# RWKV dumps and chunk loads moved from ScalarE's queue to SyncE's in a hybrid transformer block

## The chip, the cores and the metric

The kernel runs on one core of one Trainium2 chip. The metric is the device time of one execution in microseconds (us). TensorE multiplies matrices, VectorE and ScalarE do elementwise work, GpSimd a little of it, and SyncE only starts transfers. ScalarE can start transfers too: such an instruction stands in its one stream of work, between its copies and activations. Each engine takes its instructions strictly in order.

## The reference

One transformer block over 512 tokens of width 1024, in float32. A normalised input is projected by `w_in` to the inputs of three mixers and their gates; the mixers' outputs are gated, merged and projected; a gated feed-forward follows. What matters here is the projection, which is most of the matmul work, and the second mixer, RWKV-7, with 16 heads of size 64:

```python
z = h @ w_cols
zq, zf, zi, zog, zrw, zcq, zckv, zkr, zgate, zvres = jnp.split(z, IN_SPLITS, axis=-1)
o_hg = hgrn2_mixer(zq, zf, zi, zog, ...)
o_rw, v_first = rwkv7_mixer(zrw, ...)
o_mla = mla_mixer(zcq, zckv, zkr, ...)

def step(state, inp):                     # inside rwkv7_mixer, scanned over the 512 tokens
    r_t, w_t, k_t, v_t, kk_t, a_t = inp
    sa = jnp.einsum('bhvk,bhk->bhv', state, -kk_t)
    state = (state * w_t[:, :, None, :] + sa[..., None] * (kk_t * a_t)[:, :, None, :]
             + v_t[..., None] * k_t[:, :, None, :])
    return state, jnp.einsum('bhvk,bhk->bhv', state, r_t)
```

## The kernel before

**The dense stream.** Every large product goes through `stream`. Weights come in slabs of two k-tiles by 256 columns (256 KB). `slab` loads one into `wsD` on SyncE's queue, ScalarE rounds it into `whD` (L207), and VectorE takes the rest into `wlD` (`split_low`, L134). TensorE then does twelve matmuls of 128x512 on it, three for each k-tile and column block (L139 to L141), into two PSUM tiles `mmD`. Four slabs make a group; after it ScalarE copies both tiles to `zst` (L239, or L253 for the gates), and SyncE stores them (`z` or `gth`). `wsD`, `whD` and `wlD` have three buffers each, `mmD` and `zst` two. GpSimd writes a tiny `token` after every three matmuls (L151), and TensorE may not run more than five tokens ahead.

**RWKV** fills the gaps of that stream. The sequence is cut into eight chunks of 64 tokens, the heads into eight pairs, and a group is two pairs. `rwkv_group` prepares one group in a tile `G` (two buffers): `rwkv_prep` for each pair (decay scan, normalised keys, chunk-wise products, masks, transposes), `rwkv_inverse` (a recursion on VectorE), and `rwkv_merge`, whose last copies are on ScalarE (L668). Then `G` is dumped to DRAM, into `rwd`, by four transfers on ScalarE's queue (L461 and L462): 2 x (2240 + 256) KB. The next user of that buffer of `G` begins with two memsets on GpSimd (L449), which wait until the dump has landed. `rwkv_chain` comes after the fourth group and goes through the chunks in order. Chunk `c` of all groups is loaded into a tile `CH` (three buffers) by four transfers of 640 KB on ScalarE's queue (L683), one for each group. In a chunk TensorE does the products `zus` (L701, L711, L717) and `yb` (L196, L725), with copies between them on VectorE and ScalarE.

**What sets the order.** The program is written in lanes, which are priorities: the dense stream's casts and evictions are in lane 0, the chain in lane 1, the other linear mixer (HGRN, tiles `ph`, `hq`, `hk`, `hz`) in lane 2 for its products, inverse, merge and dump in lane 3, and `rwkv_prep` in lane 5. A scheduler takes, for each engine, the ready instruction of the best lane by its own estimate of times, and so writes one fixed order for each engine. `issue_after` and `add_manual_dep` add edges that it has to keep.

Of the kernel before, what the change touches and what calls it, by code (L numbers as in the profile page):

```python
# [17 lines left out]
ALU = mybir.AluOpType  # L18
# [4 lines left out]
P = 128  # L23
# [13 lines left out]
NC = S // C  # L37
# [5 lines left out]
RWC = 5 * P  # L43
# [61 lines left out]
class Kern:  # L105
# [336 lines left out]
    def rwkv_group(self, g):  # L442

        all_ = self.t(self.gp, [P, 2, NC, RWC], "G", bufs=2)
        G = self.fields(all_)
        G["all"] = all_
        for e in range(2):

            self.nc.gpsimd.memset(G["PV"][e][e * 64:e * 64 + 64], 0.0)  # L449
        G["Ld"] = self.t(self.dpool, [64, 32, 32], "Ld", bufs=2)  # L450
        G["Td"] = self.t(self.dpool, [64, 32, 32], "Td", bufs=2)
        for q in range(2):
            self.lane(5)
            self.rwkv_prep(G, 2 * g + q, q)
        self.lane(3)
        self.rwkv_inverse(G, g)
        self.rwkv_merge(G, g)
        for q in range(2):
            to = self.rwd[g][:, :, q].rearrange("c p n -> p c n")

            self.nc.scalar.dma_start(to[:, :NC - 1], all_[:, q, :NC - 1])  # L461
            self.nc.scalar.dma_start(to[:, NC - 1, :RWC - P], all_[:, q, NC - 1, :RWC - P])  # L462

    def fields(self, t):

# [3 lines left out]
    def rwkv(self, e1, e2, e3):  # L469
        self.lane(5)  # L470
        self.rwkv_lora()
        for g in range(4):
            self.rwkv_group(g)
        e2.close()
        self.rw = e1.enter_context(self.tc.tile_pool(name="rwC", bufs=1, side="right"))
        self.lane(1)
        self.rwkv_chain()
# [11 lines left out]
    def rwkv_prep(self, G, p, q):  # L489
        nc, rt = self.nc, self.rt  # L490
        V, A, Pl = nc.vector, nc.scalar, nc.gpsimd
# [15 lines left out]
        def rate(ps, tag, b):  # L507
            x = self.t(rt, [P, S], tag)
            A.activation(x, ps, AF.Tanh, bias=b[:, p:p + 1], scale=0.5)
            return x  # L510

        t1 = rate(pl[0], "t1", self.hw0)
        a = rate(pl[1], "a", self.ha0)
        lw = self.t(rt, [P, NC, C + 1], "lw")
        Pl.memset(lw[:, :, 0:1], 0.0)
        A.activation(lw[:, :, 1:], c3(t1), AF.Copy, bias=-0.5 * DECAY, scale=-0.5 * DECAY)
        cs = self.t(rt, [P, NC, C + 1], "cs")
        V.tensor_tensor_scan(cs.rearrange("p c j -> p (c j)"), self.keep, lw.rearrange("p c j -> p (c j)"),
                             0.0, op0=ALU.mult, op1=ALU.add)
        V.tensor_tensor(lw, cs, cs[:, :, C:].to_broadcast([P, NC, C + 1]), op=ALU.subtract)  # L520
        ep = self.t(rt, [P, NC, C + 1], "cs")
        em = self.t(rt, [P, NC, C + 1], "em")
# [6 lines left out]
        def proj(n, tag):  # L529
            dst = self.t(rt, [P, S], tag)  # L530
            self.shifted(dst, 8 * n + p)
            return dst

        k = proj(1, "k")
        kk, sq = self.t(rt, [P, S], "lw"), self.t(rt, [P, S], "t1")
# [10 lines left out]
        pb = self.t(self.pR, [P, NT, P], "pr")  # L546
# [2 lines left out]
        for i in range(NT):  # L549
            nc.tensor.transpose(pb[:, i, :], rb[:, 2 * i:2 * i + 2].rearrange("t h d -> t (h d)"), self.ident)  # L550
        pb = pb.rearrange("p i t -> p (i t)")
        V.tensor_tensor(kk, kk, pb, op=ALU.mult)

        BK = self.t(rt, [P, NC, P], "BK")
        X = G["X"]
# [1 line left out]
            V.scalar_tensor_tensor(X[e][H[e], q, :, 0:C], c3(kk)[H[e]], -1.0, ep[H[e], :, 0:C], op0=ALU.mult, op1=ALU.mult)  # L557
        V.scalar_tensor_tensor(kk, a, 1.0, kk, op0=ALU.add, op1=ALU.mult)
        A.activation(a, a, AF.Identity, bias=self.omka[:, p:p + 1], scale=self.hka[:, p:p + 1])
        V.tensor_tensor(k, k, a, op=ALU.mult)  # L560
        for e in range(2):
            V.scalar_tensor_tensor(BK[H[e], :, e * C:(e + 1) * C], c3(kk)[H[e]], 0.5, em[H[e], :, 1:], op0=ALU.mult, op1=ALU.mult)
            V.tensor_tensor(BK[H[e], :, (1 - e) * C:(2 - e) * C], c3(k)[H[e]], em[H[e], :, 1:], op=ALU.mult)
# [21 lines left out]
        n = NC - 1  # L585
# [7 lines left out]
        v = proj(2, "v")  # L593
        rkk = self.t(rt, [P, S], "t1")
        V.scalar_tensor_tensor(rkk, r, self.vec("rwkv_r_k", p), k, op0=ALU.mult, op1=ALU.mult)
        ps = self.t(self.pR, [P, S], "pr")
# [2 lines left out]
        self.split_low(rl, rkk, rh)  # L599
        nc.tensor.matmul(ps, lhsT=self.bdR, rhs=rh, start=True, stop=False)  # L600
        nc.tensor.matmul(ps, lhsT=self.bdR, rhs=rl, start=False, stop=True)
        V.tensor_tensor(rkk, ps, v, op=ALU.mult)
        nc.sync.dma_start(self.bv[p], rkk)

        lh, ll = self.lora_w(((slice(0, P), ins["rwkv_g_up"][0, :, f]),))
        ps = self.t(self.pR, [P, S], "pr")
        self.mm3(ps, lh, ll, self.zg[:, 0], self.zg[:, 1], True, True)
        g = self.t(rt, [P, S], "v")
# [61 lines left out]
    def rwkv_chain(self):  # L670

        nc, rw = self.nc, self.rw
        V, A, Pl = nc.vector, nc.scalar, nc.gpsimd
        mm = nc.tensor.matmul
        H = [slice(0, 64), slice(64, 128)]
        heads = [(p, e) for p in range(8) for e in range(2)]
        chunks = []

        def load(c):
            t = self.t(rw, [P, 8, RWC], "CH", bufs=3)  # L680
            n = RWC if c < NC - 1 else RWC - P
            for g in range(4):
                nc.scalar.dma_start(t[:, 2 * g:2 * g + 2, :n], self.rwd[g][c][:, :, :n])  # L683
            chunks.append(self.fields(t))

        load(0)
        St = self.t(rw, [P, 8, C], "St")
        y = self.t(rw, [P, NT, 8, 2, C], "y")
        for c in range(NC):
            if c < NC - 1:  # L690
                load(c + 1)
            G = chunks[c]
            X, PV, LM, BKT = (G[n] for n in ("X", "PV", "LM", "BKT"))
            if 0 < c < NC - 1:

                for e in range(2):
                    Pl.tensor_tensor(St[H[e]], PV[e][H[e]], self.gC[H[e], :, c + 1:c + 2].to_broadcast([64, 8, C]), op=ALU.mult)
            yo = (H[c % 2], H[1 - c % 2])
            z = self.t(self.pC, [P, 8, C], "zus")
            for p, e in heads:  # L700
                mm(z[H[e], p, :], lhsT=X[e][:, p, 0:C], rhs=PV[e][:, p, :], start=True, stop=True)  # L701
            zsb = self.t(rw, [P, 8, C], "zsb")
            V.tensor_copy(zsb, z)
            yb = self.t(self.pY, [P, 8, C], "yb")

            self.side_by_side(
                partial(mm, yb[yo[e], p, :], lhsT=X[e][:, p, C:], rhs=PV[e][:, p, :], start=p == 0, stop=False)
                for p, e in heads)
            z = self.t(self.pC, [P, 8, C], "zus")
            for p, e in heads:  # L710
                mm(z[H[e], p, :], lhsT=LM[H[e], p, 0:C], rhs=zsb[H[e], p, :], start=True, stop=True)  # L711
            V.tensor_copy(PV[0][H[0]], z[H[0]])
            A.copy(PV[1][H[1]], z[H[1]])
            if c < NC - 1:
                z = self.t(self.pC, [P, 8, C], "zus")
                for p, e in heads:
                    mm(z[H[e], p, :], lhsT=BKT[:, p, H[e]], rhs=PV[e][:, p, :], start=True, stop=True)  # L717
                for e in range(2):
                    nxt = chunks[c + 1]["PV"][e][H[e]]
                    if c == 0:  # L720
                        V.tensor_copy(nxt, z[H[e]])
                    else:
                        V.tensor_tensor(nxt, z[H[e]], St[H[e]], op=ALU.add)
            for p, e in heads:
                mm(yb[yo[e], p, :], lhsT=LM[H[e], p, C:], rhs=PV[e][H[e], p, :], start=False, stop=p == 7)  # L725
            for e in range(2):
                A.copy(y[yo[e], c // 2, :, e, :], yb[yo[e]])
            if c % 2:
                self.lane(3)
                self.rwkv_norm(y[:, c // 2].rearrange("t p e d -> t (p e) d"))  # L730
                self.lane(1)
        self.lane(3)

        bv, gr, out = (self.t(rw, [P, 8, RWC], "CH", bufs=3) for _ in range(3))
        for p in range(8):
            nc.sync.dma_start(bv[:, p, :S], self.bv[p])
            nc.sync.dma_start(gr[:, p, :S], self.grw[p])
        for p in range(8):
            pt = self.t(self.pC if p % 2 else self.pY, [P, S], "zus" if p % 2 else "yb")
            for i in range(NT):  # L740
                nc.tensor.transpose(pt[:, i * P:(i + 1) * P], y[:, i, p].rearrange("t e d -> t (e d)"), self.ident)
            o = out[:, p, :S]
            o4 = o.rearrange("f (i j t) -> f i j t", j=2, t=C)
            pt4 = pt.rearrange("f (i j t) -> f i j t", j=2, t=C)
            lb, lg = self.vec("rwkv_lnx_b", p), self.vec("rwkv_lnx_g", p)
            A.activation(o[H[0]], pt[H[0]], AF.Identity, bias=lb[H[0]], scale=lg[H[0]])
            for j in range(2):

                A.activation(o4[H[1], :, j, :], pt4[H[1], :, 1 - j, :], AF.Identity, bias=lb[H[1]], scale=lg[H[1]])
            V.tensor_tensor(o, o, bv[:, p, :S], op=ALU.add)  # L750
            V.tensor_tensor(o, o, gr[:, p, :S], op=ALU.mult)
            nc.sync.dma_start(self.orw[p], o)
            self.dump(f"orw{p}", o)
# [591 lines left out]
```

## Time and profile before

| | us |
|---|---|
| median of 3 runs | 1435.62 (1430.45 to 1436.62) |
| the profiled execution | 1436.18 |
| its span | 1434.4 |
| TensorE busy | 1364.7 (95%) |
| VectorE, ScalarE, GpSimd busy | 853.0, 637.4, 166.4 |
| data moved | 235.80 MB, mean 164 GB/s |

The profiled execution lies 0.6 us above the median and takes 1.8 us more than its span. An engine that starts a transfer is not counted as busy: such a row bears the engine's name with a q (ACTq, SPq), and its duration is the time for which the instruction held the engine. The time to landing, from the issue until the data has arrived, is another number. In rows of waits there follow the total, the count and the longest. In rows of windows there follow each engine's busy time with its count of instructions, then the clock granted to TensorE (1.00 is full), the busy share of the 16 DMA engines and GB/s. Rows of a timeline or of the chain begin with the start and the duration; brackets give the engine's idle time before the instruction and what ended it.

### The profile page before, as it was taken

What the parts mean: (1) busy time and instruction counts of PE and PEld (TensorE: products, weight loads), DVE (VectorE), ACT (ScalarE), POOL (GpSimd) and SP (SyncE); (2) the same over time, 40 slices, a digit from 0 to 9 for tenths busy, and PEclk for the clock granted to TensorE, in tenths of its full rate; (3) what the DMA queues carried; (4) which work ended last, traced back from release to release, by engine and by line L of the source; (5) the groups of instructions that cost most, each with busy time, mean ns of one, the idle gap of its engine ahead of it and who ended that gap; (6) DMA issues with size and microseconds to landing.
All of it is one profiled execution on the core that took longest, in us unless ns stands there. A gap on an engine that the chain in (4) does not pass through costs nothing.

```text
span 1434.4 us, 27281 instructions
## 1 busy us (share of the span) xinstructions
PE 1364.7 (95%) x9664; PEld 1106.5 (77%) x9664; DVE 853.0 (59%) x1756; ACT 637.4 (44%) x1259; POOL 166.4 (12%) x1000
## 2 busy tenths in 40 slices
PE   7999998998999899799999999999999999999998
PEld 6777767676776677688787878887878888888886
DVE  5566887795887784365667366665465444443234
ACT  5563555555455443234565444453344333332222
POOL 3112112111111111132210000000010000000000
PEclk9999999999999999899999999999999999999999
DMA  6564466546654748887647465403645333335333
GB/s 191 145 183 130 136 175 234 169 149 207 212 167 136 250 142 272 329 275 257 224 143 234 133 191 158 156 25 126 205 134 149 99 96 96 96 97 158 97 96 103
DMA packets 186168, 235.80 MB, mean 164 GB/s; under 512 B 33840, under 2 KB 126512, under 8 KB 186032
## 3 DMA queue, kind: packets, MB, share of 16 engines
q1 hardware_dynamic: 171072, 190.02, 43.9%
q10 hardware_dynamic: 14960, 44.05, 8.3%
q8 instruction: 76, 1.25, 0.4%
q14 instruction: 60, 0.49, 0.1%
HBM read 171.75 MB, written 62.26 MB: 163 GB/s over the span
## 4 chain that ended last, share of the span: by engine, by line
PE 75%; DMA 9%; DVE 6%; ACT 4%; issue 3%; ACTq 1%; SPq 1%; POOL 0%; DVEq 0%; POOLq 0%
PE mmD L139 17%; PE mmD L140 16%; PE mmD L141 16%; PE po L140 4%; PE po L141 4%; PE po L139 4%; DMA z<-zst 1%; DMA hz<-z 1%; DMA rwd<-G 1%; DMA zr<-z 1%; PE pm L139 1%; PE pm L140 1%; PE pm L141 1%; PE pr L196 1%; PE pmo L1117 1%
## 5 line engine op out<-in xcount | busy, mean ns | idle before, releaser
L139 PE MATMUL mmD<-xH,whD 128*128 128x512 f32 (+1 forms) x1232 | 489.6, 400 | 20.7 <-ACT zst L239 6.3
L140 PE MATMUL mmD<-xL,whD 128*128 128x512 f32 (+1 forms) x1232 | 476.6, 388 | 0.0
L141 PE MATMUL mmD<-xH,wlD 128*128 128x512 f32 (+1 forms) x1232 | 471.7, 387 | 1.5 <-DVE wlD L134 1.4
L134 DVE TENSOR_TENSOR wlD<-wsD,whD 128x512 fp32r<-128x512 f32 x384 | 264.0, 690 | 303.9 <-ACT whD L207 285.5
L207 ACT CAST whD<-wsD 128x512 fp32r<-128x512 f32 x384 | 236.4, 618 | 352.7 <-PE mmD L140 206.5
L139 PEld LDWEIGHTS mmD<-xH,whD 128*128 128x128 f32 x1232 | 233.1, 190 | 74.7 <-issue 15.6
L141 PEld LDWEIGHTS mmD<-xH,wlD 128*128 128x128 f32 x1232 | 233.7, 190 | 50.3 <-DVE wlD L134 3.0
L140 PEld LDWEIGHTS mmD<-xL,whD 128*128 128x128 f32 x1232 | 235.1, 191 | 40.4
L151 POOL MEMSET token<- 1x1 f32 x912 | 82.1, 90 | 754.3 <-PE mmD L141 739.2
L141 PE MATMUL po<-whD,fL 128*128 128x512 f32 x176 | 68.6, 390 | 0.0
L140 PE MATMUL po<-wlD,fH 128*128 128x512 f32 x176 | 68.6, 390 | 0.0
L139 PE MATMUL po<-whD,fH 128*128 128x512 f32 x176 | 62.0, 390 | 0.0
L281 POOL TENSOR_TENSOR rrs<-rtm,mhalf 128x1 f32<-128x1 f32 x8 | 4.4, 550 | 402.3 <-DVE rtm L276 368.7
L636 DVE TENSOR_TENSOR invtmp<-inv 64x30 f32<-64x30 f32 (+14 forms) x120 | 39.7, 331 | 16.2 <-DMA inv<-Ld 14.3
L239 ACT COPY zst<-mmD 128x512 f32<-128x512 f32 x64 | 37.4, 584 | 15.8 <-PE mmD L141 15.5
L637 DVE TENSOR_TENSOR inv<-inv,invtmp 64x30 f32<-64x30 f32 (+14 forms) x120 | 38.4, 320 | 2.0
L139 PEld LDWEIGHTS po<-whD,fH 128*128 128x128 f32 x176 | 33.0, 188 | 7.1
L141 PEld LDWEIGHTS po<-whD,fL 128*128 128x128 f32 x176 | 33.0, 188 | 7.0
L140 PEld LDWEIGHTS po<-wlD,fH 128*128 128x128 f32 x176 | 33.0, 188 | 7.0
L822 PEld LDWEIGHTS ph<-hq,hk 128*32 128x32 f32 x1536 | 16.8, 112 | 18.3 <-issue 8.9
L1115 ACT COPY mpT<-pmt 128x128 f32<-128x128 f32 (+3 forms) x32 | 13.6, 425 | 29.2 <-PE pmt L1113 28.9
L1117 PEld LDWEIGHTS pmo<-mpT,mv 128*128 128x128 f32 x160 | 22.3, 191 | 4.7 <-ACT mpT L1115 2.6
(349 smaller groups left out, 1964.4 us busy)
## 6 DMA issues: line engine op xcount, KB each, us to landing
wsD<-in_w_in_dram SPq DMA_DIRECT2D x176, 256.0 KB, 3.1
wsD<-in_w_ffn_in_dram SPq DMA_DIRECT2D x96, 256.0 KB, 2.8
rwd<-G ACTq DMA_DIRECT2D x8, 2240.0 KB, 11.6
CH<-rwd ACTq DMA_DIRECT2D x28, 640.0 KB, 8.4
z<-zst SPq DMA_DIRECT2D x63, 256.0 KB, 3.2
wsD<-in_w_branch_dram SPq DMA_DIRECT2D x48, 256.0 KB, 3.0
wsD<-in_w_ffn_out_dram SPq DMA_DIRECT2D x44, 256.0 KB, 2.6
zr<-z SPq DMA_DIRECT2D x26, 256.0 KB, 3.5
```

Source lines behind the costliest of these rows:

```text
L134: (eng or self.nc.vector).tensor_tensor(dst, src, high.bitcast(F32), op=ALU.subtract)
L139: first = mm(ps, lhsT=lh, rhs=rh, start=start, stop=False)
L140: mm(ps, lhsT=lh, rhs=rl, start=False, stop=False)
L141: return first, mm(ps, lhsT=ll, rhs=rh, start=False, stop=stop)
L151: token = self.nc.gpsimd.memset(self.token, 0.0).ins
L196: last = c()
L207: nc.scalar.copy(h, st)
L239: self.nc.scalar.copy(st[:m], ps)
L636: V.tensor_tensor(tv, cv, rv, op=ALU.mult)
L637: V.tensor_tensor(U[:, :j, j + 1:], U[:, :j, j + 1:], tv, op=ALU.add)
L822: mm(g[b:b + HB, o // P, :], lhsT=k[:, t], rhs=q[:, t], start=True, stop=True)
L1117: mm(pq[:, t], lhsT=self.v[:, j, h, :], rhs=pT[:, j * P:(j + 1) * P], start=j == 0, stop=j == i)
```

## The change

The dump of a group is cut into its eight chunks, of 640 KB each (512 KB for the last), and goes to SyncE's queue. The chunks are put into a list. Four places of `rwkv_prep` (the decay scan, two products on the way to the keys, and the bonus product) take one chunk from the list and issue its transfer behind an edge from that VectorE instruction; two pairs make eight such places for each group. The fourth group has no successor, so its chunks are issued at once. The loads of the chain go to SyncE's queue as well. The bytes are the same.

```diff
         self.rwkv_merge(G, g)
-        for q in range(2):
-            to = self.rwd[g][:, :, q].rearrange("c p n -> p c n")
-
-            self.nc.scalar.dma_start(to[:, :NC - 1], all_[:, q, :NC - 1])
-            self.nc.scalar.dma_start(to[:, NC - 1, :RWC - P], all_[:, q, NC - 1, :RWC - P])
+        for c in range(NC):
+            n = RWC if c < NC - 1 else RWC - P
+            self.dumps.append((self.rwd[g][c][:, :, :n], all_[:, :, c, :n]))
+        if g == 3:
+            while self.dumps:
+                self.nc.sync.dma_start(*self.dumps.pop(0))
+
+    def dump_step(self, by):
+
+        if self.dumps:
+            cur = self.cur_lane
+            self.lane(3)
+            d = self.nc.sync.dma_start(*self.dumps.pop(0))
+            self.lane(cur)
+            self.tc.add_manual_dep(d.ins, by.ins.name, mybir.DependencyInfo(
+                mybir.DependencyClass.Sync, mybir.DependencyReason.DATA), reason="spread")
...
+        at = V.tensor_tensor_scan(cs.rearrange("p c j -> p (c j)"), self.keep, lw.rearrange("p c j -> p (c j)"),
                              0.0, op0=ALU.mult, op1=ALU.add)
+        self.dump_step(at)
...
+        self.dump_step(V.tensor_tensor(kk, kk, pb, op=ALU.mult))
...
+        self.dump_step(V.tensor_tensor(k, k, a, op=ALU.mult))
...
+        self.dump_step(V.tensor_tensor(rkk, ps, v, op=ALU.mult))
...
             for g in range(4):
-                nc.scalar.dma_start(t[:, 2 * g:2 * g + 2, :n], self.rwd[g][c][:, :, :n])
+                nc.sync.dma_start(t[:, 2 * g:2 * g + 2, :n], self.rwd[g][c][:, :, :n])
```

The scheduler's order moves with it, mostly from the first dump on. In the rows that follow, a number behind a name tells one use of a buffer from the next: `wsD_1787` is a slab, cast to `whD_1789`.

ScalarE at the first group's merge, before:

```order
206 L668 COPY G_4682<-yb_5072 32x16x32 x2
207 L207 CAST whD_1723<-wsD_1721 128x512
208 L461 DMA rwd_770_4651<-G_4682 128x7x640
209 L462 DMA rwd_770_4651<-G_4682 128x512
...
212 L841 COPY hsc_4661<-ph_7852 32x4x32 x2
213 L559 ACTIVATE a_5324<-a_5324,omka,hka 128x512
214 L207 CAST whD_1745<-wsD_1743 128x512
215 L239 COPY zst_1711<-mmD_1621 128x512
```

and in the change:

```order
206 L681 COPY G_4682<-yb_5072 32x16x32 x2
207 L207 CAST whD_1723<-wsD_1721 128x512
208 L854 COPY hsc_4661<-ph_7868 32x4x32 x2
209 L572 ACTIVATE a_5324<-a_5324,omka,hka 128x512
210 L207 CAST whD_1745<-wsD_1743 128x512
211 L239 COPY zst_1711<-mmD_1621 128x512
```

The transfers (the pair at 208 and 209 comes twice) are gone from between the merge and the eviction to `zst`; all else stands in the same order.

SyncE at the same place, in the change:

```order
151 L203 DMA wsD_1743<-in_w_in_dram 128x2x256
152 L203 DMA wsD_1765<-in_w_in_dram 128x2x256
153 L470 DMA rwd_770_4651<-G_4682 256x1x640 x6
154 L203 DMA wsD_1787<-in_w_in_dram 128x2x256
155 L241 DMA z_1713<-zst_1711 128x512
156 L470 DMA rwd_770_4651<-G_4682 256x1x640
157 L203 DMA wsD_1819<-in_w_in_dram 128x2x256
```

Six of the eight chunks stand together ahead of slab 1787, since the places of the first pair, and one of the second, lie before the merge; the seventh follows soon after, and the eighth fifteen rows further on. For the second and third groups five stand together.

SyncE after the fourth group's merge, before:

```order
346 L203 DMA wsD_3699<-in_w_in_dram 128x2x256
347 L203 DMA wsD_3721<-in_w_in_dram 128x2x256
348 L203 DMA wsD_3743<-in_w_in_dram 128x2x256
349 L203 DMA wsD_3773<-in_w_in_dram 128x2x256
350 L254 DMA gth<-zst_3669 128x512
351 L254 DMA gth<-zst_3672 128x512
352 L203 DMA wsD_3795<-in_w_in_dram 128x2x256
```

and in the change, where the 12 loads of the first three chunks are the rows 368 to 379:

```order
360 L203 DMA wsD_3699<-in_w_in_dram 128x2x256
361 L463 DMA rwd_773_4654<-G_6081 256x1x640 x7
362 L463 DMA rwd_773_4654<-G_6081 256x1x512
363 L203 DMA wsD_3721<-in_w_in_dram 128x2x256
364 L203 DMA wsD_3743<-in_w_in_dram 128x2x256
365 L203 DMA wsD_3773<-in_w_in_dram 128x2x256
366 L254 DMA gth<-zst_3669 128x512
367 L254 DMA gth<-zst_3672 128x512
368 L696 DMA CH_6562<-rwd_770_4651 128x1280
...
379 L696 DMA CH_6666<-rwd_773_4654 128x1280
380 L203 DMA wsD_3795<-in_w_in_dram 128x2x256
```

Slab 3721 now stands behind the last dump, and slab 3795 behind twelve chunk loads.

TensorE where it first needs slab 3795 (cast to `whD_3797`), in the change:

```order
2203 L816 MATMUL ph_9082<-cst,hz_9080 128x128 x4
2204 L724 MATMUL zus_6610<-zsb_6591,CH_6562 64x64 x16
2205 L738 MATMUL yb_6593<-CH_6562 64x64
2206 L730 MATMUL zus_6629<-CH_6562 64x64 x16
2207 L738 MATMUL yb_6593<-CH_6562 64x64 x15
2208 L714 MATMUL zus_6673<-CH_6569 64x64 x16
2209 L193 MATMUL yb_6692<-CH_6569 64x64
2210 L196 MATMUL yb_6692<-CH_6569 64x64 x15
2211 L724 MATMUL zus_6709<-zsb_6690,CH_6569 64x64 x16
2212 L139 MATMUL mmD_3771<-xH_9_110,whD_3797 128x512
```

Before, that slab began right after the first chunk's L711; now the rest of chunk 0 and half of chunk 1 come ahead of it, with no dense matmul between them.

More of the change, by code (lines that the diff above doesn't have):

```diff
@@ L471, in rwkv @@
         self.rwkv_lora()
+        self.dumps = []
         for g in range(4):
@@ L517, in rwkv_prep @@
         cs = self.t(rt, [P, NC, C + 1], "cs")
-        V.tensor_tensor_scan(cs.rearrange("p c j -> p (c j)"), self.keep, lw.rearrange("p c j -> p (c j)"),
+        at = V.tensor_tensor_scan(cs.rearrange("p c j -> p (c j)"), self.keep, lw.rearrange("p c j -> p (c j)"),
                              0.0, op0=ALU.mult, op1=ALU.add)
+        self.dump_step(at)
         V.tensor_tensor(lw, cs, cs[:, :, C:].to_broadcast([P, NC, C + 1]), op=ALU.subtract)
@@ L551, in rwkv_prep @@
         pb = pb.rearrange("p i t -> p (i t)")
-        V.tensor_tensor(kk, kk, pb, op=ALU.mult)
+        self.dump_step(V.tensor_tensor(kk, kk, pb, op=ALU.mult))
         BK = self.t(rt, [P, NC, P], "BK")
@@ L559, in rwkv_prep @@
         A.activation(a, a, AF.Identity, bias=self.omka[:, p:p + 1], scale=self.hka[:, p:p + 1])
-        V.tensor_tensor(k, k, a, op=ALU.mult)
+        self.dump_step(V.tensor_tensor(k, k, a, op=ALU.mult))
         for e in range(2):
@@ L601, in rwkv_prep @@
         nc.tensor.matmul(ps, lhsT=self.bdR, rhs=rl, start=False, stop=True)
-        V.tensor_tensor(rkk, ps, v, op=ALU.mult)
+        self.dump_step(V.tensor_tensor(rkk, ps, v, op=ALU.mult))
         nc.sync.dma_start(self.bv[p], rkk)
```

## The prediction

> **What bounds the kernel now.** First the page's busy shares and its chain:
>
> ```profile
> span 1434.4 us, 27281 instructions
> PE 1364.7 (95%) x9664; PEld 1106.5 (77%) x9664; DVE 853.0 (59%) x1756; ACT 637.4 (44%) x1259; POOL 166.4 (12%) x1000
> PE 75%; DMA 9%; DVE 6%; ACT 4%; issue 3%; ACTq 1%; SPq 1%; POOL 0%; DVEq 0%; POOLq 0%
> ```
>
> TensorE is the bound: all its idle time is about 70 us of 1434.4, and no change to transfers can bring more. So the question is how much of that idle time sits at the dumps and chunk loads. The waits, asked for one stretch around each dump, then for the whole span:
>
> ```profile
> PE mmD L139 <- ACT zst L239: 2.8, 1, 2.8
> ...
> PE pr L550 <- ACT t L548: 1.7, 1, 1.7
> ...
> PE pr L550 <- ACT t L548: 2.9, 1, 2.9
> ...
> ACT zst L253 <- DMA CH<-rwd: 9.7, 1, 9.7
> ...
> ACT whD L207 <- DMA rwd<-G: 5.6, 1, 5.6
> ...
> PE mmD L139 <- ACT whD L207: 4.2, 1, 4.2
> ...
> PE mmD L139 <- ACT zst L253: 3.5, 1, 3.5
> ...
> PE pr L550 <- ACT t L548: 6.2, 4, 2.9
> ```
>
> In order: the first dump (222 to 240 us), the second (340 to 360), the third (466 to 490), the fourth with the chunk loads (560 to 605, four rows), the whole span. TensorE always waits for ScalarE, and the two rows of ACT say why that was late at the fourth: its first chunk load waited until the dump had landed (5.6), and the next ones held it (9.7). ScalarE's timeline shows the rest:
>
> ```profile
> 227.84 3.66 ACTq L462 DMA_DIRECT2D rwd<-G  x1
> 231.54 0.52 ACT L841 COPY hsc<-ph 32x128 f32<-32x128 f32 x2 [5.33 <-PE ph L839]
> 474.44 4.42 ACTq L462 DMA_DIRECT2D rwd<-G  x1
> 582.16 10.23 ACTq L683 DMA_DIRECT2D CH<-rwd  x5
> ```
>
> The fourth issue of a dump holds ScalarE 3.66 or 4.42 us, five chunk loads hold it 10.23 us, and casts and evictions queue behind. ScalarE's 5.33 us are put down to a matmul that was long done; the time is that of the issues.
>
> Each such pause costs more than its length, since TensorE comes back at a lower clock:
>
> ```profile
> 560.23 0.39 PE L139 MATMUL mmD<-xH,whD 128*128 128x512 f32 x1
> 560.46 0.39 PE L140 MATMUL mmD<-xL,whD 128*128 128x512 f32 x1
> 582.63 0.63 PE L140 MATMUL mmD<-xL,whD 128*128 128x512 f32 x1
> 583.06 0.63 PE L141 MATMUL mmD<-xH,wlD 128*128 128x512 f32 x1
> 560.00:570.00 10.00, 10.00 (x118) 7.58 (x116) 3.91 (x9) 3.83 (x10) 1.15 (x13) 1.00 0.96 347
> 570.00:580.00 10.00, 7.00 (x46) 5.33 (x39) 1.52 (x4) 1.18 (x4) 0.71 (x9) 0.95 0.79 308
> 580.00:590.00 10.00, 8.49 (x40) 6.57 (x40) 1.99 (x3) 1.76 (x3) 0.70 (x8) 0.71 0.96 358
> 590.00:600.00 10.00, 6.76 (x60) 5.21 (x62) 3.49 (x12) 3.23 (x6) 0.47 (x3) 0.83 1.03 405
> ```
>
> Matmuls start 0.23 us apart at full clock and 0.43 us apart after a pause (granted clock 0.71 and 0.83 in those windows). A count of slow matmuls gives 9 after the first dump, 10 and 6 after the last two pauses, some 5 after the third dump: 1.7, 2.1, 1.4 and 1.5 us with the transposes there.
>
> **What goes.** All 16 dump issues and 32 chunk loads leave ScalarE.
> - First dump: 2.8 + 1.7 = 4.5 us.
> - Second: the wait at L550 is 1.7. Four such waits sum to 6.2, so the two that no dump delays average (6.2 - 1.7 - 2.9) / 2 = 0.8, and 0.9 goes.
> - Third: 2.9 - 0.8 + 1.5 = 3.6 us.
> - Fourth dump and loads: 4.2 + 2.1 + 3.5 + 1.4 = 11.2 us.
>
> Together 20.2 us.
>
> **What is added.** SyncE issues 32 dump chunks and 32 loads. Their issue delays nothing but what stands behind them in its order, so what matters is which slab that is. Rates come from the windows: 308 to 347 GB/s while a dump ran, 358 to 405 for chunk loads. Landing times of slabs (`wsD`) between 500 and 545 us, from 560 to 580 beside a dump, and from 580 to 600 beside chunk loads, all on the other queue:
>
> ```profile
> DMA to landing us min/median/max: 2.5/2.9/4.1
> ...
> DMA to landing us min/median/max: 7.2/8.8/8.9
> ...
> DMA to landing us min/median/max: 9.5/12.6/13.6
> ```
>
> How late may a slab land? A slab of twelve matmuls lasts 12 x 0.23 = 2.8 us. A load is issued when the slab three before it has been split, which can be cast once TensorE is done with the one six before: five slabs, 14 us, lie between. Cast and split take 1.3 us, once at each end:
>
> ```profile
> L134 DVE TENSOR_TENSOR wlD<-wsD,whD 128x512 fp32r<-128x512 f32 x384 | 264.0, 690 | 303.9 <-ACT whD L207 285.5
> L207 ACT CAST whD<-wsD 128x512 fp32r<-128x512 f32 x384 | 236.4, 618 | 352.7 <-PE mmD L140 206.5
> ```
>
> So a landing of up to 14 - 2.6 = 11.4 us is covered.
>
> *First three dumps.* Five or six chunks stand together: 3.28 or 3.93 MB, 9.5 to 12.8 us at 308 to 347 GB/s, and then the slab's own 2.9. That is 12.4 to 15.7, partly over the cover; but the burst starts at the merge, with five to six slabs (14 to 17 us) and the preparation's own products still ahead of TensorE. I take 1 us for each dump (bounds 0 and 3), 3 in all. The later chunks come singly (under 2.2 us each) and are covered.
>
> *The wait for VectorE.* A chunk tied to a step keeps SyncE, and the slabs behind it, until that VectorE instruction is done. The fourth step costs nothing new: the store of `bv` right behind waits for the same instruction. The second and third are on the path to the keys, which no longer waits for ScalarE. I take 0 (bounds 0 and 2), with the 11.4 us as cover.
>
> *The buffer of G.* The last chunk leaves later than the old dump, and the memsets on GpSimd wait for it with the pacing tokens behind them:
>
> ```profile
> 367.88 0.95 POOL L449 MEMSET G<- 64x1024 f32 x1 [1.85 <-DMA wsD<-in_w_in_dram]
> ```
>
> That wait of 1.85 us cost TensorE nothing, as five tokens are 15 matmuls or 3.5 us. Twice 0.5 us (bounds 0 and 3): 1 us.
>
> *Fourth dump.* Eight chunks, 5.1 MB, 14.7 to 16.6 us. Six slabs, 16.8 us, and some HGRN products are ahead: covered, so the 4.2 us pause goes.
>
> *Chunk loads.* SyncE waits until the dump has landed, then issues twelve loads (7.86 MB, 19.4 to 22 us at 405 to 358 GB/s) ahead of slab 3795. With issue, landing and cast it is ready 23 to 25 us after the dump. TensorE meanwhile has the end of slab 3701 and slabs 3721, 3743 and 3773 (9 to 10 us), HGRN (2), and chunk work at these durations:
>
> ```profile
> 602.21 1.08 PE zus L711 x32
> 614.33 0.82 PE yb L196 x28
> ```
>
> Six sets of 1.08 and two of 0.82 are 8.1 us: 19 to 20 us of work against 23 to 25, so 3 to 6 us idle, split over waits for the copies between the sets and for the slab. I take 4, and 2 for the low clock: 6 (bounds 2 and 12). Later each chunk puts only 2.6 MB, 6.5 to 7.3 us, ahead of a slab: with 2.9 that is 10.2 at most, inside 11.4.
>
> **Sum.** -20.2 + 3 + 0 + 1 + 6 = -10.2. The profiled execution took 1436.2, so 1426.0; it lies 0.6 above the median of 1435.62, which becomes 1425.4. I say 1426. Half a percent, 7.2 us, is about what a measurement of this kernel can tell from no change.
>
> The Trainium skill, DMA: Bandwidth & Descriptors, section Issuing engines are not separate DMA queues, says that transfers of all issuers run on the same 16 engines and that a second issuer only saves the sequencer's time, usually small beside the transfer. By that rule the sum would be near 0, and it is the first rival; the held 3.66, 4.42 and 10.23 us speak against it here.
>
> **Rivals.**
> *No change: the transfers set the pauses, not their issue.* For it: the DMA share is 0.79 to 1.03 from 560 to 600 us. Against it: in the same stretch ScalarE, not a late slab, ends both of TensorE's waits. Then the first three dumps give back half (9.0 / 2 = 4.5), minus 2 for the bursts, and the fourth gives nothing: 1436 - 2.5 = 1433.5.
>
> *Slower: slabs queue behind the chunk loads.* If the one queue moves only 308 GB/s, the twelve loads take 25.5 us and slab 3795 comes 9 us late, 11 with the clock; nothing is won at the fourth dump. Each of the five later sets of four loads takes 8.5 us, and its first load also waits for a free `CH` buffer with slabs behind it. It decides once landing passes 11.4 us; at 3 us over, five sets cost 15. With the first three dumps at 9.0 - 6: 1436.2 + 15 - 3 = 1448. For it: slabs took 9.5 to 13.6 us beside chunk loads even on a queue of their own. Against it: 405 GB/s in 590 to 600.
> The Trainium skill, same page, section Queues, rings and completion order, lets a DMA engine take queue rows in turn but one row's descriptors in ring order, which speaks for this rival; no run yet shows the order within a row.
>
> *The change doesn't spread.* The order shows it already: five, six or eight chunks together. It is in the sums above.
>
> **Chances.** Forecast 0.5 (0.45 of it faster); no change 0.3 (0.03 faster); slower 0.15; the rest 0.05, a longer hold of the tokens or a worse order elsewhere (0.02 slower). So faster 0.48, same 0.35, slower 0.17. The range 1414 to 1441 goes from nearly all 20.2 us won to the no-change case plus its bounds (3 more at the bursts, 3 at GpSimd); it leaves out most of the slower rival. The forecast's own range is 1416 to 1434.
>
> **What would show it.** Right: no ACTq rows for `rwd` and `CH`; no wait of TensorE on L239, L207 or L253 over 2 us near a dump; one pause of 3 to 6 us where slab 3795 starts; the low clock there alone. Wrong: `wsD` landing above 11.4 us more than once, SPq waits on VectorE at the dumps that end in TensorE's waits, or POOL's L449 with more than 3.5 us before it.

## The result, and the profile after

| | before | after | ratio (95% interval) |
|---|---|---|---|
| median, us | 1435.62 (1430.45 to 1436.62) | 1426.14 (1420.9 to 1427.52) | 0.9923 (0.99 to 0.9946) |
| medians in another session (e5) | 1436.36 | 1425.90 | 0.9916 (0.9901 to 0.9931) |
| profiled execution, its span | 1436.18, 1434.4 | 1427.17, 1425.4 | |

The forecast was 1426.0. The total came out; this part shows that the two halves of its sum did not. From the page of the changed kernel (span, busy times, shares of the chain), then its transfers on SyncE in the timeline (start, time for which the issues held SyncE):

```profile
span 1425.4 us, 27298 instructions
PE 1365.3 (96%) x9664; PEld 1110.6 (78%) x9664; DVE 853.2 (60%) x1756; ACT 638.5 (45%) x1259; POOL 165.6 (12%) x1000
PE 74%; DMA 10%; DVE 8%; ACT 4%; issue 3%; SPq 1%; POOL 0%; DVEq 0%; POOLq 0%; ACTq 0%
```

```profile
227.17 6.73 SPq L470 DMA_DIRECT2D rwd<-G  x6
...
345.10 5.99 SPq L470 DMA_DIRECT2D rwd<-G  x5
...
471.23 5.48 SPq L470 DMA_DIRECT2D rwd<-G  x5
...
555.06 9.99 SPq L463 DMA_DIRECT2D rwd<-G  x8
...
571.28 11.27 SPq L696 DMA_DIRECT2D CH<-rwd  x12
```

The five or six chunk issues at a merge hold SyncE 5.5 to 6.7 us, about 1.1 us each; before, the four issues of a whole dump held ScalarE 5.0 to 6.4 us. The twelve loads take 0.9 us each here; five of them on ScalarE took 10.23 us before. ACTq has gone from the chain (1% before), and TensorE's busy time is the same (1364.7): the gain is idle time (60.1 us of the span, 69.7 before). TensorE's waits around the second dump (340 to 360 us), the third (466 to 490) and the fourth with the chunk loads (555 to 625); around the first (220 to 260) there is none of 0.2 us or more:

```profile
PE pr L563 <- ACT t L561: 2.3, 1, 2.3
PE mmD L139 <- ACT zst L239: 1.4, 1, 1.4
PE ph L835 <- DVE ss L556: 1.1, 1, 1.1
...
PE pr L553 <- ACT t L549: 0.4, 1, 0.4
PE ph L896 <- ACT hkT L893: 0.3, 1, 0.3
...
PE zus L724 <- DVE zsb L716: 2.2, 1, 2.2
PE yb L738 <- DVE CH L725: 0.8, 1, 0.8
PE mmD L139 <- ACT whD L207: 0.6, 1, 0.6
PE zus L714 <- PE yb L738: 0.5, 1, 0.5
PE zus L730 <- ACT CH L726: 0.3, 1, 0.3
```

Before, they were 2.8 + 0.9 at the first dump, 1.7 + 1.5 + 0.9 at the second, 2.9 at the third and 4.2 + 3.5 at the fourth (lines behind the edit lie 13 lower in this kernel: L550 before is L563 here). So the second dump has not become better: 4.1 us before, 4.8 now. The two rows of 2.2 and 0.6 us at the fourth belong to different places: 0.6 is slab 3795 at 596 us, and 2.2 comes 15 us later. Slabs issued from 553 to 572 us (beside the dump) and from 571 to 590 (behind twelve chunk loads) landed as follows:

```profile
DMA to landing us min/median/max: 3.1/5.8/6.8
...
DMA to landing us min/median/max: 10.8/11.1/11.4
```

The wait of 2.2 us, for VectorE's copy to `zsb` at 611 us, is a late slab's too. ScalarE's timeline there:

```profile
607.37 1.38 ACT L207 CAST whD<-wsD 128x512 fp32r<-128x512 f32 x2 [3.31 <-DMA wsD<-in_w_in_dram]
```

ScalarE waited 3.31 us for two slabs that stood behind four chunk loads and landed 8.6 to 9.1 us after their issue. VectorE in turn waited 2.7 us for these casts, and the copy stands behind the two splits in its order.

Two things look worse. GpSimd waits for the last chunk of a dump before it may clear the next `G`, and TensorE for a token behind that. First the two rows of GpSimd's timeline, then TensorE's waits from 255 to 300 us:

```profile
266.83 1.94 POOL L449 MEMSET G<- 64x1024 f32 x2 [6.25 <-DMA rwd<-G]
...
389.41 1.94 POOL L449 MEMSET G<- 64x1024 f32 x2 [3.04 <-DMA rwd<-G]
...
PE mmD L139 <- POOL token L151: 2.7, 1, 2.7
PE pr L627 <- DVE t L615: 0.7, 1, 0.7
```

### The profile page after: what moved, and what is told of

Same layout as the page of the kernel before. It is cut to its first block, busy times and chain, and to the rows that moved or that the text cites. A ratio compares the mean times of both kernels' runs of the same rounds, so it can differ in the third digit from the quotient of the medians.

```text
span 1425.4 us, 27298 instructions
## 1 busy us (share of the span) xinstructions
PE 1365.3 (96%) x9664; PEld 1110.6 (78%) x9664; DVE 853.2 (60%) x1756; ACT 638.5 (45%) x1259; POOL 165.6 (12%) x1000
## 4 chain that ended last, share of the span: by engine, by line
PE 74%; DMA 10%; DVE 8%; ACT 4%; issue 3%; SPq 1%; POOL 0%; DVEq 0%; POOLq 0%; ACTq 0%
PE mmD L139 17%; PE mmD L140 16%; PE mmD L141 16%; PE po L139 3%; PE po L141 3%; PE po L140 3%; DVE wlD L134 1%; DMA wsD<-in_w_in_dram 1%; PE pm L139 1%; PE pm L140 1%; PE pm L141 1%; PE pmo L1130 1%; DMA zr<-z 1%; PE pr L196 1%; DMA z<-zst 1%
## 5 line engine op out<-in xcount | busy, mean ns | idle before, releaser
L139 PE MATMUL mmD<-xH,whD 128*128 128x512 f32 (+1 forms) x1232 | 488.0, 398 | 11.5 <-POOL token L151 5.0
L207 ACT CAST whD<-wsD 128x512 fp32r<-128x512 f32 x384 | 236.8, 618 | 363.9 <-PE mmD L140 227.7
L835 PE MATMUL ph<-hq,hk 128*32 128x32 f32 x1536 | 23.3, 200 | 5.4 <-DVE hk L860 3.1
L1121 ACT ACTIVATE mp<-pm,mmx,scq 128x128 f32<-128x128 f32 (+3 forms) x32 | 19.8, 620 | 18.9 <-DVE mmx L1118 18.8
```

The costliest lines, as they stand in the source:

```text
L139: first = mm(ps, lhsT=lh, rhs=rh, start=start, stop=False)
L207: nc.scalar.copy(h, st)
L835: mm(g[b:b + HB, o // P, :], lhsT=k[:, t], rhs=q[:, t], start=True, stop=True)
L1121: A.activation(p[:, :n], s_, AF.Exp, bias=mx, scale=self.scq[:, i:i + 1], accum_out=sm)
```

## The experiments

The first view of after suggested that the sum was right with one term too small (the buffer of `G`). The theory to test: what the change saves is ScalarE's hold by issues, place by place. The main rival: the spreading, not the engine, does it.

| kernel | first three dumps | fourth dump | chunk loads | ratio to before | TensorE idle, 400 to 520 us |
|---|---|---|---|---|---|
| before | whole, ScalarE | whole, ScalarE | ScalarE | 1 | 9.57 |
| e2 | whole, ScalarE | whole, ScalarE | SyncE | 0.9987 (0.997 to 1.0004) | 9.47 |
| e8 | whole, ScalarE | chunks, SyncE | SyncE | 0.9985 (0.9973 to 0.9997) | 9.22 |
| e3 | whole, SyncE | whole, SyncE | SyncE | 0.9968 (0.9954 to 0.9983) | 7.68 |
| e10 | chunks, untied, SyncE | chunks, SyncE | SyncE | 0.9958 (0.9943 to 0.9974) | 10.21 |
| e12 | only the third tied, SyncE | chunks, SyncE | SyncE | 0.9952 (0.9934 to 0.997) | 11.55 |
| e11 | only the first two tied, SyncE | chunks, SyncE | SyncE | 0.993 (0.9915 to 0.9946) | 6.09 |
| e6 | tied, ScalarE | chunks, ScalarE | SyncE | 0.9946 (0.9924 to 0.9967) | 4.61 |
| e7 | tied, SyncE | whole, ScalarE | ScalarE | 0.9934 (0.992 to 0.9948) | 3.63 |
| e1 | tied, SyncE | chunks, SyncE | ScalarE | 0.9957 (0.9936 to 0.9979) | 4.07 |
| e9 | tied, SyncE | whole, SyncE | SyncE | 0.9932 (0.991 to 0.9955) | 4.41 |
| e4 | tied, SyncE, later memset | chunks, SyncE | SyncE | 0.9951 (0.9929 to 0.9973) | 5.73 |
| after | tied, SyncE | chunks, SyncE | SyncE | 0.9923 (0.99 to 0.9946) | 5.52 |
| e5 (after again) | | | | 0.9916 (0.9901 to 0.9931) | 5.11 |

The last column is 120 us less the PE time in the row of windows for that stretch of each kernel's profile. Each profile is of one execution, and executions of one kernel differ by 5 us and more, so a profile tells where, and the ratio how much.

**e1, the loads back on ScalarE.**

```diff
-                nc.sync.dma_start(t[:, 2 * g:2 * g + 2, :n], self.rwd[g][c][:, :, :n])
+                nc.scalar.dma_start(t[:, 2 * g:2 * g + 2, :n], self.rwd[g][c][:, :, :n])
```

> The change with the chunk loads back on ScalarE's queue; the dumps stay as changed. Theory (what the change saves is ScalarE's hold by issues, place by place): the stretch to 560 us keeps its gain (in the profile of after some 4.6 us less idle and slow time at the first dump, 6.1 at the third, less 4.5 given back by the hold at G's memset and by the wait at the second dump, so 6 net), and the stretch 560 to 640 us gets back the pauses of the kernel before (5 to 8 us): 1436 - 6 + 1 = 1429 to 1432. Rival (the whole gain is in the loads): 1435 to 1437. Rival (the loads cost as much on SyncE as they save, the dumps alone give it all): 1424 to 1427. ScalarE's rows for the loads should show issues of 8 to 10 us in a row again and TensorE waiting on L253 or L207 over 2 us.

Median 1428.89. Much as the theory had it: the gain without the loads is about 6 us (3 to 9), and ScalarE's hold by the loads is back. That the loads are worth the rest does not follow: e7 below has them on ScalarE too, with the fourth dump, and is 9.5 us better than before; the two intervals overlap. The waits of e1, TensorE's from 555 to 625 us and ScalarE's over the span:

```profile
PE mmD L139 <- ACT zst L253: 5.3, 1, 5.3
...
ACT zst L253 <- DMA CH<-rwd: 11.6, 1, 11.6
```

**e2, the kernel before with the loads alone on SyncE** (the same line, the other way).

> The kernel before with the chunk loads alone moved to SyncE's queue; the dumps stay whole, on ScalarE. Theory: the stretch to 560 us is as before, the pause behind the fourth dump on ScalarE (4.2 us at L207) stays or shrinks, the one behind the loads (3.5 us at L253 and its low clock) goes and slab 3795 comes late by some us: 1429 to 1433. Rival (the whole gain is in the loads): 1425 to 1428. Rival (SyncE held by loads delays the slabs behind, no gain): 1434 to 1438, with landing of wsD past 11.4 us.

Median 1434.60; by the ratio 1.9 us less, with no change inside the interval. The loads alone bring almost nothing, as the last rival had it. Both pauses for ScalarE (4.2 and 3.5) are gone, and in their place TensorE waits for a late slab (waits of e2 over the whole span: two on L207, the longest 4.1):

```profile
PE mmD L139 <- ACT whD L207: 5.4, 2, 4.1
```

The three slabs behind the twelve loads landed 11.2 to 13.1 us after their issue: past the 11.4 us that the prediction counts as covered, and here TensorE does wait. Another 3.6 us of shorter waits from 555 to 625 us lie mostly between the chain's steps.

**e3, whole dumps at the merge, but on SyncE.**

```diff
-        for c in range(NC):
-            n = RWC if c < NC - 1 else RWC - P
-            self.dumps.append((self.rwd[g][c][:, :, :n], all_[:, :, c, :n]))
-        if g == 3:
-            while self.dumps:
-                self.nc.sync.dma_start(*self.dumps.pop(0))
+        for q in range(2):
+            to = self.rwd[g][:, :, q].rearrange("c p n -> p c n")
+            self.nc.sync.dma_start(to[:, :NC - 1], all_[:, q, :NC - 1])
+            self.nc.sync.dma_start(to[:, NC - 1, :RWC - P], all_[:, q, NC - 1, :RWC - P])
```

> The change with its dumps as before in form (four transfers for each group, all at the merge, no tie to a step), but issued on SyncE; chunk loads on SyncE. Theory (only the issuing engine matters, and the last chunk's lateness costs 4 to 7 us through G's memset on GpSimd): that hold is gone (no row of L449 with over 1 us before it) and the rest is as in after: 1420 to 1424. Rival (spreading shields the slabs from the dump's bytes): slabs land after 11 us at each merge and TensorE waits for L207: 1430 to 1438. Rival (neither matters): 1426.

Median 1430.79: the theory failed here. ScalarE is free, GpSimd's hold at L449 is down to 1.10 and 0.72 us, TensorE's pause at the first dump is gone, and still it is 4.6 us better than before, not 11 or more. The rival's reason is not seen either: TensorE waits for L207 only 1.8 us in the whole span.

**e4, the memset later.** The two memsets of `G` for groups 2 and 3 are tied to the scan of their own preparation:

```diff
+        if p in (4, 6):
+            for e in range(2):
+                m = Pl.memset(G["PV"][e][e * 64:e * 64 + 64], 0.0)
+                self.tc.add_manual_dep(m.ins, at.ins.name, ...)
```

> The change, with the two memsets of G's zero half for groups 2 and 3 tied to the scan of their own preparation, so that GpSimd gets to them 7 us (the first) and some 2 us (the second) later, when the last dump chunk has landed. Theory: the 6.25 and 3.04 us that GpSimd waited at L449 go, with TensorE's 2.75 us on the token, the 3.4 us of slow matmuls at 270 to 280 us, and perhaps part of the wait at the second dump: 1421 to 1424. Rival (those pauses are made up later, or come from elsewhere): 1426 to 1427, with the same idle and slow time at 260 to 300 us.

Median 1428.34: the waits before the memset went (6.25 and 3.04 to 0.69 and 0.33), and nothing was won. TensorE's waits from 255 to 300 us in e4:

```profile
PE mmD L139 <- ACT zst L239: 2.3, 1, 2.3
PE ph L840 <- DVE hk L865: 0.8, 1, 0.8
PE pr L632 <- DVE t L620: 0.7, 1, 0.7
```

Where it had waited 2.7 us for the token, it now waits 2.3 for an eviction. The scheduler also wrote another order for TensorE behind that place (some 100 rows differ), so how much of the remaining difference to the changed kernel is its doing stays open.

**e5, the changed kernel again**, beside the next three.

> The changed kernel itself, unaltered, beside the next three on one chip: a measure to set the others against. It gave 0.9923 (0.99 to 0.9946) of the kernel before: 1424 to 1428. If it comes out at 0.995 or above, the differences of some 3 us between it and the kernels with whole dumps or a later memset are those of chips, not of kernels.

1425.90, ratio 0.9916: the ratio repeats within 0.1%, about 1 us. One ratio's interval still spans 3 to 6 us, so neighbours in the table are not told apart.

**e6, chunks tied to steps, issued by ScalarE** (`self.nc.scalar` for `self.nc.sync` in the two places that issue `self.dumps.pop(0)`).

> The change with the dump chunks still cut and tied to steps, but issued by ScalarE; chunk loads on SyncE. Theory (what matters is which engine is held by the issues): five to eight chunk issues at each merge hold ScalarE 4 to 8 us, TensorE waits at L239, L207 or L563 as in the kernel before, and only the loads' own gain is left: 1432 to 1436. Rival (spreading the bytes is what helps, the issuer does not matter): 1425 to 1428.

Median 1429.73, between theory and rival. At the first dump the theory holds to the letter: four of the chunk issues hold ScalarE 4.13 us, and TensorE waits again (e6, ScalarE's timeline and TensorE's wait from 222 to 240 us):

```profile
226.51 4.13 ACTq L470 DMA_DIRECT2D rwd<-G  x4
...
PE mmD L139 <- ACT zst L239: 3.7, 1, 3.7
```

And yet the kernel is 6 us better than e2, which issues the same bytes whole from the same engine. With e3 and the changed kernel this makes a square (all four dumps whole or in chunks, on either engine): for the dumps, the engine is worth 0.2 to 0.3% (e2 to e3, e6 to after), tying the chunks 0.4 to 0.5% (e2 to e6, e3 to after). The intervals of e2 and e3 overlap, and so do those of e6 and the changed kernel, so the engine's share is at the edge of what these runs tell. Every such edit changes TensorE's order as well: these are prices of edits, not yet of causes.

**e7 and e8, the two halves of the change**: e7 has only the first three dumps changed, e8 only the fourth dump and the loads.

In short:

```diff
 e7: +        if g < 3:
              (chunks into the list, as in the change)
     +        else:
     +            (the four whole transfers on ScalarE; loads on ScalarE)
 e8: +        if g < 3:
     +            (the four whole transfers on ScalarE)
     +        else:
     +            (eight chunks on SyncE; loads on SyncE)
```

> The change for the first three dumps alone: the fourth dump whole on ScalarE and the chunk loads on ScalarE, as before. The prediction's terms give -9.0 + 3 + 1 = -5 us against the kernel before: 1429 to 1432. If the spread dumps carry most of the gain (the dumps without the loads gave -6 to -7 us): 1428 to 1430. Rival (the fourth dump and the loads carry it all): 1434 to 1437.

> The other half: the first three dumps whole on ScalarE as before, the fourth dump chunk by chunk and the chunk loads on SyncE. The prediction's terms give -11.2 + 6 = -5 us: 1429 to 1432. The loads alone gave -1 to -2 us; if the fourth dump's issues on ScalarE were what kept them from more, the two together give 4 us or more. Rival (the stretch from 560 to 690 us is bound by the slabs behind the loads, whoever issues): 1433 to 1436.

Medians 1428.10 and 1434.69. By the ratios, e7 is 9.5 us better than before (7.5 to 11.5) and e8 2.2 (0.4 to 3.9); the prediction had 5.0 and 5.2. They add to 11.7, and the changed kernel in the same session (e5) is 12.1 better. Why e8 gains little, TensorE's waits from 555 to 625 us in e8:

```profile
PE yb L741 <- DVE CH L728: 1.7, 2, 0.9
PE zus L727 <- DVE zsb L719: 1.6, 1, 1.6
PE mmD L139 <- ACT whD L207: 0.9, 1, 0.9
PE ph L879 <- ACT hkT L876: 0.6, 1, 0.6
PE zus L717 <- PE yb L741: 0.5, 1, 0.5
```

Without the dense matmuls between them, the chain's steps wait for the copies between them: with three more rows (0.3, 0.2, 0.2) these are 6.0 us, for 7.7 before: a gain of 1.7.

**e9, the fourth dump whole on SyncE**, all else as in the change.

> The change with the fourth dump alone as before in form: four transfers instead of eight chunks, on SyncE; first three dumps spread, chunk loads on SyncE. SyncE would be held some 5 us for it instead of 9.99. Theory (the gain of the first three dumps adds to that of the flush, and the fewer issues let the chunk loads start earlier): the idle time between 550 and 690 us falls from 4.5 us to some 2.6, as in the kernel with all dumps whole on SyncE, and the time is 1422 to 1425. Rival (the flush is bound by its bytes): no difference to the changed kernel, 1424 to 1428.

Median 1427.13, the rival: no difference.

**e10, all chunks at the merge, none tied** (`if g == 3:` becomes `if True:`).

> The change with all eight chunks of each dump at the merge on SyncE, none tied to a step; chunk loads on SyncE. So the cut is kept and the spread taken away (of the change's eight chunks five or six already stood together). Theory A (the ties matter: two or three chunks that leave later let slabs through, and the planner, which counts a dump's time, orders the preparation behind the third merge otherwise): it loses what the whole dumps on SyncE lost, 1429 to 1432. Theory B (the cut into chunks matters, not the ties): 1424 to 1428.

Median 1431.31, theory A: cut but untied is like whole (e3). TensorE's order is the same in e3 and e10, row for row, and the same in after and e9; between the two orders some 500 of 5,600 rows differ, all behind the first dump. Measured side by side, e9 is 0.26% faster than e10, some 4 us. The last column of the table says where it tells. PE busy (second number) from 400 to 520 us in before, e10, after and e6:

```profile
400.00:520.00 120.00, 110.43 (x1053) 85.53 (x1052) 92.06 (x204) 58.66 (x119) 17.85 (x114) 0.99 0.58 181
...
400.00:520.00 120.00, 109.79 (x1044) 84.31 (x1043) 91.30 (x206) 60.03 (x121) 18.42 (x116) 0.97 0.58 183
...
400.00:520.00 120.00, 114.48 (x1079) 89.05 (x1079) 97.19 (x221) 63.72 (x125) 18.95 (x125) 1.00 0.60 187
...
400.00:520.00 120.00, 115.39 (x1086) 89.82 (x1085) 96.85 (x219) 63.89 (x129) 18.85 (x128) 1.00 0.61 189
```

The 14 profiles fall into two classes without overlap: 7.68 to 11.55 us idle (mean 9.6) where the first two dumps are not tied, 3.63 to 6.09 (mean 4.9) where they are, whichever engine issues. The DMA share is alike. The longest waits there, in e10:

```profile
PE pr L193 <- DVE G L591: 3.0, 2, 1.8
PE mmD L139 <- POOL token L151: 2.7, 2, 1.7
PE pr L553 <- ACT t L549: 1.6, 2, 1.3
```

None of them ends with a transfer. But this stretch is not the whole account. From 225 to 400 us it is the tied kernels that idle more (8.6, 9.3 and 11.5 us in after, e5 and e9, against 7.0 and 7.2 in e10 and e3), and over the whole span TensorE idles 60.1, 57.9 and 63.6 us in the three and 62.0 and 62.6 in the two. So the stretch shows where the orders part, and the gain of the ties can't be read from it alone.

**e11 and e12, ties for some dumps only** (`if g > 1:` and `if g != 2:` in that place).

> All dumps in chunks on SyncE; those of the first two groups tied to steps as in the change, those of the third and fourth all at the merge. With every tie taken away the time was 1431, with all of them 1426. Theory A (a tie helps by the bytes that leave later, at its own dump): two of three dumps tied give two thirds, 1427.5 to 1429, and only the third dump shows a pause like the untied kernel's. Theory B (ties help because the planner writes another order for all that follows, also where no dump runs): no such proportion; the idle time between slabs 102 and 126 (some 408 to 515 us) and 174 and 192 (740 to 820 us) goes either with the untied kernel's (10 us in the two) or with the changed kernel's (some 3 us), and the time with it, 1430 to 1432 or 1425 to 1427.

> The complement: only the third group's dump tied to steps, the others in chunks at the merge, all on SyncE. Theory A (bytes that leave later, dump by dump): one third of the ties' 5 us, 1429 to 1430.5. Theory B (the planner's order): as before, all or nothing by the idle time at 408 to 515 us and 740 to 820 us: 1430 to 1432 or 1425 to 1427.

Medians 1426.96 and 1429.71. By the times alone the two theories are hardly apart; the place tells. The third dump begins at some 470 us. It is untied in e11 and tied in e12, so by theory A e11 should pause there and e12 not. TensorE's waits from 460 to 490 us, e10, e11, e12:

```profile
PE mmD L139 <- POOL token L151: 1.7, 1, 1.7
PE pr L553 <- ACT t L549: 1.3, 1, 1.3
```

```profile
PE ph L896 <- ACT hkT L893: 0.5, 1, 0.5
PE pr L553 <- ACT t L549: 0.4, 1, 0.4
```

```profile
PE mmD L139 <- POOL token L151: 3.1, 1, 3.1
PE pr L553 <- ACT t L549: 0.9, 1, 0.9
```

It is the other way round. TensorE's order in e11 is that of after, and in e12 that of e10, until some 490 us, past the third dump. GpSimd's timeline there, e12, then e11, shows one piece of it:

```profile
469.23 2.02 POOL L281 TENSOR_TENSOR rs<-ss,mhalf 128x8 f32<-128x8 f32 x1 [3.52 <-DVE htm L276]
471.20 0.09 POOL L151 MEMSET token<- 1x1 f32 x1
471.26 1.00 POOL L281 TENSOR_TENSOR hrs<-htm,mhalf 128x4 f32<-128x4 f32 x1
```

```profile
462.76 1.02 POOL L281 TENSOR_TENSOR hrs<-htm,mhalf 128x4 f32<-128x4 f32 x1 [5.17 <-DVE htm L276]
463.72 0.53 POOL L151 MEMSET token<- 1x1 f32 x4
...
470.19 1.64 POOL L281 TENSOR_TENSOR rs<-ss,mhalf 128x8 f32<-128x8 f32 x1 [5.42 <-DVE ss L556]
```

In e12 (as in e10 and e3) the norm of the keys `rs` stands ahead of HGRN's `hrs`; GpSimd waits for VectorE and then works on it 2.02 us, and the token that TensorE needs stands behind. In e11 (as in after) `hrs` and four tokens come first. Of theory B one part fell: from 740 to 820 us e12, at 1430 in all, has after's short waits (0.41 us idle; e10 3.42, after 0.45), so this piece does not go with the first two ties. That the order, and not the later departure of the chunks, makes the time is argued: e3 and e10 share an order and a time, after and e9 do too, and none of the long waits of e10 from 400 to 520 us ends with a transfer; but no run has the changed kernel's order without its ties.

## Why the prediction came out right

**ScalarE's hold by issues: right as a mechanism, small as a price.** The pause at the first dump is there in every kernel that dumps from ScalarE (2.8, e2 2.8, e8 2.9, e6 3.7) and in none that dumps from SyncE. But in time all issues on SyncE, with no ties, are worth 4.6 and 6.0 us (e3, e10), of which the dumps' engine is 0.2 to 0.3%, 3 to 4 us. The sum took 20.2 us away for the issues and added 10 back. The rule of the Trainium skill, DMA: Bandwidth & Descriptors, section Issuing engines are not separate DMA queues, that a second issuer saves only the sequencer's time, usually small, comes nearer to these 3 to 4 us than the prediction's discount of it; near zero, as the first rival read it, it is not.

**First three dumps: -5.0 foreseen, -9.5 measured (e7).** Two terms were mis-sized, and one was missing. The bursts on SyncE were put at 3: slabs beside the first three dumps landed in 6.6 us at most, under the 11.4 of cover, and no wait of TensorE there ends with a late slab, so 0. The wait for VectorE, put at 0, shows none either. The buffer of `G` was put at 1: the two holds were longer than foreseen, over the 3.5 us that was to prove the step wrong in one of the two, but taking them away (e4) won nothing. What was missing is a price for the ties. The text treated the ties as a matter of SyncE's queue and bytes, and the rival "the change doesn't spread" as settled because five or six chunks stay together. By that step a tied dump is no better than an untied one; measured, the ties bring 0.3 to 0.5%, 4 to 7 us. They go with another order of the scheduler's, and the idle time parts most plainly between 400 and 520 us (4.7 us, some of it given back before and behind); that the order is the cause is argued, as said above. The term for the third dump, 3.6, lies in this stretch, but the issue was not its cause: e6 issues from ScalarE there and has 4.61 us idle against 9.57 before, and e3 issues from SyncE and has 7.68.

**Second dump: 0.9 was to go.** It didn't: the wait at L550, 1.7, is one of 2.3 at L563 now. So the issue did not set it, as at the third.

**Fourth dump and loads: -5.2 foreseen, -2.2 measured (e8).** The idle part looks near in the changed kernel: 4.2 + 3.5 went and 4.4 came, where 4 was forecast. But only 2.2 of it (0.8, 0.3, 0.5 and 0.6) lies at slab 3795, split as foreseen over the copies between the chain's sets and the slab. What failed is the clock in it (3.5 us gone, 2 added) and, in e8, 1.6 us more of waits than in the changed kernel, between the chain's steps. The other 2.2 comes at 611 us, from slabs behind a later set of four loads. The prediction put those sets at nothing, since 10.2 us at most is inside the 11.4 of cover; they landed in 8.6 to 9.1 us and still held a copy of the chain, through VectorE's order, which the cover leaves out.

**The low clock.** The sum let 6.7 us of slow matmuls go and 2 come. One less the granted clock, times the span, is 19.2 us on average over 77 executions of before and 18.0 over 11 of after (each has a spread of 3): no gain of that size. The slow stretches move; they do not go. In the changed kernel's profile the windows of 10 us with a granted clock under 0.9 include those from 270 (0.66), 350 (0.66), 610 (0.83) and 690 us (0.50), so "the low clock there alone" was wrong too.

**The rivals.** No change was refuted twice over (0.9923, 0.9916). Slower had its condition measured: behind twelve chunk loads the slabs took 10.8 to 11.4 us, at the cover's edge and not past it, and TensorE waited 0.6 us for one itself and 2.2 behind two later ones. In e2, where they took up to 13.1 us, it waited 4.1. The rule behind that rival (the Trainium skill, DMA: Bandwidth & Descriptors, section Queues, rings and completion order: one row's descriptors in ring order) agrees with these landings as far as they go; no run here separates a row's order from the bytes ahead.

The total was right by luck, because errors cancelled: 4.5 us too little for the first three dumps, 3 too much for the fourth and the loads. What in the scheduler's reckoning turns a tie into the better order, and whether that order could be had without ties, stays open. No kernel of the study is faster than the changed one.

## What to carry to other kernels

Where a scheduler writes the order, an edge that holds a transfer back can also change the order of every engine behind it, as here: compare the orders far from the place of the edit, and price the waits there, before pricing the transfer. A hold on an engine is worth its pause only as far as the next wait does not stand right behind it. Here the issues' move to SyncE alone (e3, e10) brought 4.6 and 6.0 us of the 15 that the rows of waits at the dumps showed. And a sum that hits the total proves none of its terms: run the halves.

## What the runs showed of the hardware

The issue of a 640 KB chunk held SyncE about as long as ScalarE in a burst, 1.0 to 1.2 us each (SyncE: 5.48 to 5.99 us for five, 9.99 for eight; ScalarE in e6: 4.13 for four), so the cost moves with the instruction. Loads differ more: twelve held SyncE 11.27 us, five held ScalarE 10.23 before. And the loss by the lower granted clock stayed at 17 to 20 us on average in each of the kernels, whichever pauses they had, where I had expected it to go with the pauses.
